# The first MLP product of a two-block layer by seven quarter products instead of eight

## The chip, the core and the metric

The kernel runs on one core of a Trainium2 chip. The metric is device time in microseconds (us) of one execution. The core has a matrix engine (TensorE, here PE), VectorE (DVE), ScalarE (ACT), GpSimd (POOL) and queues of DMA transfers, here all issued by SyncE (SP). Each engine takes its instructions in a fixed order; semaphores make one wait for another.

## What is computed

Two blocks on x of 1024 tokens by 1024 channels, all in fp32. The part around the change is the MLP of block 1 and what follows it:

```python
h = rms_norm(x, g_mlp[l])
f = jnp.square(jax.nn.relu(jnp.einsum("bsd,df->bsf", h, w_1[l])))   # 1024 -> 4096
x = x + jnp.einsum("bsf,fd->bsd", f, w_2[l])                         # 4096 -> 1024
...
x = rms_norm(x, g_final)                                             # end of block 1
...
h = rmsnorm(x, norm_g[l]); proj = h @ w_in[l]                        # block 2
...
mn = rmsnorm(mem, mem_norm_g); kv = mn @ w_kv                        # memory attention, 256 rows of mem
```

## The kernel before

Activations lie with channels on the 128 partitions and tokens along the free axis, in two halves of 512 tokens (`hf`). Every fp32 matrix product is made of three passes in a 22-bit form of fp32: each operand is split into a high part H (rounded, by ACT) and a low part L (the rest, by DVE), and L·H, H·L and H·H are summed in PSUM. So a tile of 128 output channels by 512 tokens with a contraction of 1024 takes 8 x 3 = 24 matmuls of 128x128 on 128x512.

`weight` (L101 on) loads a weight tile of 128x1024 (512 KB, L106) into one of two staging buffers `wst`, has ACT write its high part `wh` (L108) and DVE its low part `wl` (L110); four `wh` and four `wl` buffers turn. `split` does the same for activations (ACT L131, DVE L132). `mm3` issues the matmuls: all cross passes first (L124), then H·H (L127), or operand by operand when `ordered` (L119). Accumulators in PSUM have the tags `pm` and `pa`, four buffers each.

`out_proj` ends with the RMS norm of the MLP's input, half by half: squares (ACT L152), their sum over tiles (DVE L155), the sum over partitions by two matmuls (`spread`, L167 and L168), the reciprocal root (`rsqrt`: ACT L176, L179, DVE L181, L184, L186), then `scaled`: for each of eight channel tiles one multiplication (DVE L194) and a split into the pages `acth` and `actl`.

`mlp` runs over eight groups `e` of 512 inner channels. For each half it makes four tiles of the first product, takes relu out of PSUM on ACT (L636), squares on DVE (L638) and splits into the pages `e0` to `e7`; then, with four tiles of `w_2`, 16 output tiles of 12 matmuls, each added to x on DVE (L648). In the last group the sums of squares for the norms of block 1's end and block 2's start follow each add (L152, L155), and after each half come the norm, the scaled and split input of block 2, and, at low priority, x scaled and written to DRAM (L660, L661). Ahead of group 6 `mem_norm` (its sums at L882, its scaling at L873) normalizes the memory rows; the kv product of those rows (weights `w_kv`) stands after the MLP and before the projection of block 2.

A list scheduler fixes the order of each engine's instructions by priorities: weights are given the place they would have 185 instructions earlier (`W_AHEAD`), the relu and the adds are moved up by 500 (`urgent`), the writing of x back by 300 (`LATE`). Where buffers of a tag are all in use, an instruction waits for the last reader of the oldest.

Of the kernel before, what the change touches and what calls it, by code (L numbers as in the profile page):

```python
# [61 lines left out]
class Builder:  # L62
# [36 lines left out]
    def urgent(self):  # L99
        return self.tc.high_priority(offset=URGENT)  # L100

# [490 lines left out]
    def out_proj(self, mx):  # L592
        nc, V = self.nc, self.nc.vector
        self.x1 = [None] * 8
        h2 = Act(KC)
        acc = [None, None]
        for b in range(2):
            ws = [self.weight(self.io["w_o"][4 * b + i]) for i in range(4)]
            for hf in range(2):
                sl = slice(hf * HALF, (hf + 1) * HALF)  # L600
                for i in range(4):
                    c = 4 * b + i
                    if hf == 0:
                        self.x1[c] = self.page(f"x{c}")
                    xr = self.load(self.io["x"][c][:, sl])
                    ps = self.ct(ws[i], mx, hf)
                    V.tensor_tensor(self.x1[c][:, sl], ps, xr, ALU.add)  # L607
                    acc[hf] = self.square_sum(acc[hf], self.x1[c][:, sl])
                if b == 1:
                    rs = self.rsqrt(self.spread(acc[hf], self.mean_d), EPS)  # L610
                    self.scaled(h2, hf, [t[:, sl] for t in self.x1], self.vec("g_mlp", 0, KC), rs)
        return h2

    def ct4(self, w, j, act, hf, first=0, cols=slice(0, HALF)):
        ps = self.psum((P, cols.stop - cols.start))
        h, l = w
        self.mm3(ps, [(h[:, j * HALF + k * P:j * HALF + (k + 1) * P], l[:, j * HALF + k * P:j * HALF + (k + 1) * P],
                       act.H(hf, first + k)[:, cols], act.L(hf, first + k)[:, cols]) for k in range(4)])
        return ps

    def mlp(self, h2):
        nc, V, A = self.nc, self.nc.vector, self.nc.scalar
        h3 = Act(KC)
        for e in range(8):
            if e == 6:
                self.mem = self.mem_norm()
            f = Act(4)
            ws = [self.weight(self.io["w_1"][4 * e + i]) for i in range(4)]
            for hf in range(2):
                for pr in range(2):  # L630
                    self.ext_pages(f, hf, pr, hf * 4 + pr)
                for i in range(4):
                    ps = self.ct(ws[i], h2, hf, e == 0 and i == 0)
                    t = self.tmp("b")
                    with self.urgent():
                        A.activation(t, ps, AF.Relu)  # L636
                    t2 = self.tmp("b")
                    V.tensor_tensor(t2, t, t, ALU.mult)  # L638
                    self.split(t2, f.H(hf, i), f.L(hf, i))
            w2 = [self.weight(self.io["w_2"][4 * e + i]) for i in range(4)]  # L640
            for hf in range(2):
                sl = slice(hf * HALF, (hf + 1) * HALF)
                acc1 = acc2 = None
                for c in range(8):
                    ps = self.ct4(w2[c // 2], c % 2, f, hf)
                    x = self.x1[c][:, sl]
                    with self.urgent():
                        V.tensor_tensor(x, ps, x, ALU.add)  # L648
                    if e == 7:
                        acc1 = self.square_sum(acc1, x)  # L650
                        acc2 = self.square_sum(acc2, x, self.vec("g_final", c))
                if e == 7:
                    V.scalar_tensor_tensor(acc2, acc1, EPS, acc2, ALU.mult, ALU.add)
                    rs = self.rsqrt(self.spread(acc2, self.mean_d), EPS * EPS)
                    self.scaled(h3, hf, [t[:, sl] for t in self.x1], self.gg, rs)
                    rs1 = self.rsqrt(self.spread(acc1, self.mean_d), EPS, out=acc1)
                    with self.tc.high_priority(offset=-LATE):
                        for c in range(8):
                            x = self.x1[c][:, sl]
                            V.scalar_tensor_tensor(x, x, self.vec("g_final", c), rs1, ALU.mult, ALU.mult)  # L660
                            nc.sync.dma_start(self.x_dram[c][hf], x)  # L661
        return h3

    def gates(self, h3):
        nc, V, A, G = self.nc, self.nc.vector, self.nc.scalar, self.nc.gpsimd
# [370 lines left out]
    def build(self):  # L1036
        tc = self.tc
        MT = bass.MemoryType
        with (
            tc.tile_pool(name="consts", bufs=1) as self.consts,  # L1040
            tc.tile_pool(name="smalls", bufs=8) as self.smalls,
            tc.tile_pool(name="wst", bufs=2) as self.wst,
            tc.tile_pool(name="wh", bufs=N_W) as self.wh,
            tc.tile_pool(name="wl", bufs=N_W) as self.wl,
            tc.tile_pool(name="pages", bufs=1) as self.pages,
            tc.tile_pool(name="rolls", bufs=N_ROLL) as self.rolls,
            ExitStack() as stack,
            tc.tile_pool(name="dram", bufs=1, space=MT.DRAM) as dram,
        ):
# [9 lines left out]
            self.x_dram = [[dt("xd", 2 * c + hf, (P, HALF)) for hf in range(2)] for c in range(8)]  # L1059
            self.rows_dram = [[dt("rows", 2 * i + hf, (4, HALF)) for hf in range(2)] for i in range(2)]  # L1060
# [12 lines left out]
LATE = 300  # L1073
URGENT = 500
CONV_STEP = 20
N_ROLL = 2
# [20 lines left out]
def _ct_groups(w):  # L1097
    k, c = w.shape
    return w.reshape(k // HALF, 4, P, c // 256, 2, P).transpose(0, 3, 2, 4, 1, 5).reshape(-1, P, 1024)


def _layout(a):
    o = {}
# [13 lines left out]
    o["w_rg"] = wr.reshape(4, P, 1024)  # L1117
    o["w_o"] = _ct(a["w_o"][0])
    o["w_1"] = _ct(a["w_1"][0])
    o["w_2"] = _ct_groups(a["w_2"][0])  # L1120
    w2 = a["w_in_2"][0]
    gates = np.zeros((D, P), np.float32)
    gates[:, 0:4] = w2[:, 2560:2564]
# [10 lines left out]
    for n, c in V_COLS:  # L1134
# [6 lines left out]
        elif n in ("conv_a_w", "conv_b_w", "conv_w_2"):  # L1141
            w = a[n][0][:, RNN_ORDER] if n == "conv_b_w" else a[n][0]
# [55 lines left out]
```

## Time and profile before

| | |
|---|---|
| median of 3 runs | 2385.77 us (2385.24 to 2388.82) |
| profiled execution, its time | 2385.94 us |
| its span in the trace | 2384.2 us |
| PE / DVE / ACT busy | 98% / 63% / 37% |
| MLP, first to last matmul | 986.69 to 1684.98 us |

Busy shares are means over stages with different limits; a stage is read from its own stretch. In a timeline, the brackets tell how long the engine stood idle before an instruction and what released it. A row that stands for several instructions (x3) shows the time from the first's start to the last's end, and these overlap somewhat: their start-to-start time is shorter than the time of one.

### The profile page before, as it was taken

The page shows a single profiled execution, that of the slowest core. Times are in us where ns is not written, and L with a number is a line of the kernel's source. Part 1 is how long each engine was busy: PE and PEld are TensorE (multiplying, and loading weights), DVE is VectorE, ACT ScalarE, POOL GpSimd, SP SyncE. Part 2 cuts the span into 40 slices and gives each one's busy share as a digit, 9 for nine tenths or more (in the row PEclk, how much of TensorE's full clock was granted, in tenths as well). Part 3 has the DMA queues.
Part 4 walks back from the last instruction along what each step waited for, and adds up shares of the span by engine and source line. Part 5 has one row for each costly group of instructions (what it writes and reads, how often), then busy time and mean ns, then how long its engine had stood idle before and what let it go on. Part 6 is the DMA issues. An engine that isn't in the chain of part 4 may idle for free.

```text
span 2384.2 us, 26982 instructions
## 1 busy us (share of the span) xinstructions
PE 2341.8 (98%) x10656; PEld 1934.1 (81%) x10656; DVE 1498.1 (63%) x2233; ACT 883.9 (37%) x1370; POOL 18.8 (1%) x44
## 2 busy tenths in 40 slices
PE   8999999999999999999999999999899999999998
PEld 6887888878878888888888888888787888888777
DVE  8999998995664234743343333435937467775866
ACT  6445463555552112422112212314614344443422
POOL 0000000000000000000000000000000000000000
PEclk9999999999999999999999999999999999999999
DMA  4223232233425223211121121111322111223421
GB/s 155 80 67 98 66 91 90 83 105 101 136 89 174 82 81 105 78 54 53 36 62 45 45 62 36 53 53 36 112 101 63 54 58 53 81 65 109 133 88 71
DMA packets 76480, 191.09 MB, mean 80 GB/s; under 512 B 9264, under 2 KB 11824, under 8 KB 76352
## 3 DMA queue, kind: packets, MB, share of 16 engines
q1 hardware_dynamic: 76352, 189.36, 25.2%
q8 instruction: 83, 1.36, 0.2%
q14 instruction: 45, 0.37, 0.1%
HBM read 153.64 MB, written 34.11 MB: 79 GB/s over the span
## 4 chain that ended last, share of the span: by engine, by line
PE 72%; DVE 9%; ACT 2%; issue 2%; DMA 1%; POOL 0%; DVEq 0%; ACTq 0%; POOLq 0%
PE pm L124 45%; PE pm L127 22%; PE pa L124 2%; DVE e L358 1%; DVE wl L110 1%; PE pa L127 1%; DMA ld<-y 1%; DVE actl L132 1%; DVE row L155 1%; ACT wh L108 0%; DVE c L194 0%; DVE x L1033 0%; ACT c L152 0%; PE pa L802 0%; PE pa L948 0%
## 5 line engine op out<-in xcount | busy, mean ns | idle before, releaser
L124 PE MATMUL pm<-acth,wl 128*128 128x512 f32 (+1 forms) x2480 | 960.2, 388 | 9.8 <-ACT b L473 5.5
L124 PE MATMUL pm<-actl,wh 128*128 128x512 f32 (+1 forms) x2480 | 960.3, 388 | 0.4 <-DVE actl L132 0.4
L127 PE MATMUL pm<-acth,wh 128*128 128x512 f32 (+1 forms) x2480 | 620.9, 387 | 0.0
L124 PEld LDWEIGHTS pm<-acth,wl 128*128 128x128 f32 x2480 | 466.7, 188 | 106.8 <-ACT b L473 6.8
L124 PEld LDWEIGHTS pm<-actl,wh 128*128 128x128 f32 x2480 | 466.9, 188 | 96.2 <-DVE actl L132 1.7
L127 PEld LDWEIGHTS pm<-acth,wh 128*128 128x128 f32 x2480 | 461.8, 188 | 93.6 <-issue 0.7
L108 ACT ACTIVATE wh<-wst 128x1024 fp32r<-128x1024 f32 x209 | 220.5, 1057 | 543.2 <-PE pm L127 516.2
L110 DVE TENSOR_TENSOR wl<-wst,wh 128x1024 fp32r<-128x1024 f32 x209 | 255.3, 1224 | 87.9 <-ACT wh L108 87.3
L124 PE MATMUL pm<-e,wl 128*128 128x512 f32 x592 | 230.4, 389 | 0.0
L124 PE MATMUL pm<-e,wh 128*128 128x512 f32 x592 | 230.3, 389 | 0.0
L648 DVE TENSOR_TENSOR x<-pm,x 128x512 f32<-128x512 f32 x128 | 88.5, 691 | 176.2 <-PE pm L127 176.1
L127 PE MATMUL pm<-e,wh 128*128 128x512 f32 x592 | 158.1, 389 | 0.0
L638 DVE TENSOR_TENSOR b<-b 128x512 f32<-128x512 f32 x64 | 44.4, 693 | 177.6 <-ACT b L636 177.6
L124 PEld LDWEIGHTS pm<-e,wl 128*128 128x128 f32 x592 | 111.1, 188 | 23.4 <-DVE wl L110 0.4
L127 PEld LDWEIGHTS pm<-e,wh 128*128 128x128 f32 x592 | 111.1, 188 | 23.1
L124 PEld LDWEIGHTS pm<-e,wh 128*128 128x128 f32 x592 | 111.1, 188 | 23.1
L358 DVE SCALAR_TENSOR_TENSOR e<-roll,pv,e 128x507 f32<-128x507 f32 (+14 forms) x174 | 120.5, 748 | 0.0
L636 ACT ACTIVATE b<-pm 128x512 f32<-128x512 f32 x64 | 38.4, 599 | 203.5 <-PE pm L127 202.7
L358 DVE SCALAR_TENSOR_TENSOR e<-roll,tap_sum,e 128x511 f32<-128x511 f32 (+14 forms) x90 | 63.2, 746 | 0.0
L152 ACT ACTIVATE c<-x 128x512 f32<-128x512 f32 (+1 forms) x63 | 36.1, 580 | 70.5 <-DVE x L607 35.0
L155 DVE TENSOR_TENSOR row<-row,c 128x512 f32<-128x512 f32 (+1 forms) x77 | 48.2, 642 | 15.6 <-ACT c L152 15.5
L579 DVE TENSOR_TENSOR b<-pm,ld 128x512 f32<-128x512 f32 x16 | 11.0, 690 | 71.7 <-PE pm L127 71.7
(313 smaller groups left out, 2301.5 us busy)
## 6 DMA issues: line engine op xcount, KB each, us to landing
wst<-in_w_in SPq DMA_DIRECT2D x89, 512.0 KB, 3.5
wst<-in_w SPq DMA_DIRECT2D x64, 512.0 KB, 3.5
sig<-b SPq DMA_DIRECT2D x32, 256.0 KB, 2.8
ld<-sig SPq DMA_DIRECT2D x32, 256.0 KB, 2.6
a<-p SPq DMA_DIRECT2D x24, 256.0 KB, 3.9
wst<-in_w_b_out SPq DMA_DIRECT2D x12, 512.0 KB, 4.2
y<-b SPq DMA_DIRECT2D x24, 256.0 KB, 2.0
wst<-in_w_out SPq DMA_DIRECT2D x12, 512.0 KB, 3.5
```

The lines of the kernel that those rows point to most:

```text
L108: nc.scalar.activation(h, st, AF.Copy)
L110: nc.vector.tensor_tensor(l, st, h.bitcast(F32), ALU.subtract)
L124: self.nc.tensor.matmul(ps, a, b, start=i == 0, stop=i == n - 1)
L127: self.nc.tensor.matmul(ps, aH, bH, start=i == 0, stop=i == n - 1)
L132: self.nc.vector.tensor_tensor(L, srcap, H.bitcast(F32), ALU.subtract)
L152: nc.scalar.activation(sq, x, AF.Square, scale=scale)
L155: (eng or nc.vector).tensor_tensor(acc, acc, sq, ALU.add)
L358: ops.append(lambda k=k: V.scalar_tensor_tensor(out[:, k:], x[:, :HALF - k], taps[k], out[:, k:], ALU.mult, ALU.add))
L579: V.tensor_tensor(t, ps, sg, ALU.mult)
L636: A.activation(t, ps, AF.Relu)
L638: V.tensor_tensor(t2, t, t, ALU.mult)
L648: V.tensor_tensor(x, ps, x, ALU.add)
```

## The change

The first 512 inner channels are done as before. The other 3584 come in 14 steps `q` of 256. In a step the first product, 256 inner channels by 1024 by 1024 tokens, is taken as a 2x2 by 2x2 block product (two tiles of channels, two halves of the contraction, two halves of the tokens) and made by seven block products of 12 matmuls instead of eight (`seven`, `product`). They need sums of the operands and of the results:

- Four sums of activation blocks, T1 to T4, 16 tiles of 128x512. They are made once, while half 1 of the normalized x is scaled (`scaled_and_sums`, six operations for each of four pairs of tiles), written to DRAM (`t_dram`, 16 tiles of 256 KB), and, during the first 512 channels, read again and split (`sum_pair`). T2 and T3 then fill the working tiles `a`, `c`, `roll` and `ld` and T1 and T4 fill pages until the last step.
- Four sums of weight blocks per step (`weight_sums`, DVE), and the high and low parts of 3584 instead of 2048 columns of `w_1` material.
- Seven combinations of the products per step, read out of PSUM by DVE, and one copy by ACT, instead of four relus by ACT. The square is one DVE operation, max(z, 0)·z.

The second product of a step has a contraction of 256: 16 output tiles of 6 matmuls, each with an add to x, where a group had 16 tiles of 12. The host stores `w_2` in another order for it. `mem_norm`, whose tiles are held by the sums, comes after the seven products of the last step. In the last step the output tiles of half 0 come before those of half 1, with the norms as before.

```diff
+    def scaled_and_sums(self, act, xs, g, rs):
...
+        def one(k):
+            ts[k] = self.tmp("c")
+            V.scalar_tensor_tensor(ts[k], xs[k], g[:, k:k + 1], rs, ALU.mult, ALU.mult)
+            self.split(ts[k], act.H(1, k), act.L(1, k))
...
+        for k in range(4):
+            one(k)
+            one(4 + k)
+            with self.tc.high_priority(offset=-SUMS_LATE):
+                t12, t22 = ts.pop(k), ts.pop(4 + k)
+                t1 = self.tmp("c")
+                V.tensor_tensor(t1, act.H(0, k).bitcast(F32), t12, ALU.subtract)
+                V.tensor_tensor(t1, t1, act.L(0, k).bitcast(F32), ALU.add)
+                nc.sync.dma_start(self.t_dram[0][k], t1)
+                V.tensor_tensor(t12, t12, t22, ALU.subtract)
+                nc.sync.dma_start(self.t_dram[2][k], t12)
+                V.tensor_tensor(t22, t22, t1, ALU.add)
+                nc.sync.dma_start(self.t_dram[1][k], t22)
+                t4 = self.tmp("c")
+                V.tensor_tensor(t4, act.H(0, 4 + k).bitcast(F32), t22, ALU.subtract)
+                V.tensor_tensor(t4, t4, act.L(0, 4 + k).bitcast(F32), ALU.add)
+                nc.sync.dma_start(self.t_dram[3][k], t4)
+    def sum_pair(self, i, k, homes):
...
+        t = self.tmp("row")
+        nc.sync.dma_start(t, self.t_dram[i][k])
+        self.split(t, homes[0], homes[1])
...
+    def weight_sums(self, s1, s0):
...
+            st1 = self.wst.tile([P, 1024], F32, tag="wst", name=self.name("wst"))
+            nc.sync.dma_start(st1, s1)
+            st0 = self.wst.tile([P, 1024], F32, tag="wst", name=self.name("wst"))
+            nc.sync.dma_start(st0, s0)
...
+            a1 = parts(st1)
+            a22 = parts(st0[:, hi], 512)
+            V.tensor_tensor(st0[:, hi], st0[:, lo], st0[:, hi], ALU.add)
+            V.tensor_tensor(st0[:, lo], st1[:, lo], st0[:, lo], ALU.add)
+            V.tensor_tensor(st1[:, lo], st0[:, hi], st1[:, lo], ALU.add)
+            V.tensor_tensor(st1[:, hi], st1[:, lo], st1[:, hi], ALU.add)
+            x24 = parts(st1)
+            x31 = parts(st0)
...
+        p1 = self.product(w["A11"], B["B11"])
...
+            A.activation(c11, p1, AF.Copy)
+        p6 = self.product(w["X2"], B["T2"])
...
+        tt(c12, c11, p6, ALU.subtract)
+        p4 = self.product(w["A22"], B["T4"])
+        p7 = self.product(w["X3"], B["T3"])
...
+        tt(c22, p7, c12, ALU.subtract)
...
+        tt(c21, p4, c22, ALU.add)
+        p5 = self.product(w["X1"], B["T1"])
+        tt(c22, c22, p5, ALU.subtract)
+        tt(c12, c12, p5, ALU.add)
+        p2 = self.product(w["A12"], B["B21"])
+        tt(c11, c11, p2, ALU.add)
+        p3 = self.product(w["X4"], B["B22"])
+        tt(c12, c12, p3, ALU.add)
...
+        for q in range(2, 16):
+            w = self.weight_sums(self.io["w_1"][2 * q], self.io["w_1"][2 * q + 1])
...
+            c11, c12, c21, c22 = self.seven(w, B)
+            self.squared(c21, None, fh[0][1], fl[0][1])
+            self.squared(c11, None, fh[0][0], fl[0][0])
+            self.squared(c22, None, fh[1][1], fl[1][1])
+            self.squared(c12, None, fh[1][0], fl[1][0])
+            if q == 15:
                 self.mem = self.mem_norm()
...
+            w2 = [self.weight(self.io["w_2"][2 * q + j]) for j in range(2)]
+            for hf, b in ((0, 0), (1, 0), (0, 1), (1, 1)) if q < 15 else ((0, 0), (0, 1), (1, 0), (1, 1)):
...
+                    x = self.add_x(c, hf, ps)
+                    if q == 15:
+                        acc[0] = self.square_sum(acc[0], x)
+                        acc[1] = self.square_sum(acc[1], x, self.vec("g_final", c))
+                if q == 15 and b == 1:
+                    self.norm2(hf, *acc)
```

Three places in the order of the engines' instructions show what moved. The first is DVE where half 1 of the normalized x is scaled; `c` are the scaled tiles and the sums, `acth` and `actl` the pages of the normalized x, `b` squares of the first group. Before:

```order
L186 SCALAR_TENSOR_TENSOR c_7627<-c_7628,c_7627 128x512
L194 SCALAR_TENSOR_TENSOR c_7636<-x_1024_7040,pv,c_7627 128x512
L194 SCALAR_TENSOR_TENSOR c_7640<-x_1028_7071,pv,c_7627 128x512
L194 SCALAR_TENSOR_TENSOR c_7646<-x_1032_7103,pv,c_7627 128x512
L132 TENSOR_TENSOR actl_1119_7635<-c_7636,acth_1118_7634 128x512
L132 TENSOR_TENSOR actl_1119_7635<-c_7640,acth_1118_7634 128x512
L132 TENSOR_TENSOR actl_1123_7645<-c_7646,acth_1122_7644 128x512
L194 SCALAR_TENSOR_TENSOR c_7650<-x_1036_7135,pv,c_7627 128x512
```

After:

```order
L626 SCALAR_TENSOR_TENSOR c_7658<-x_1024_7056,pv,c_7643 128x512
L626 SCALAR_TENSOR_TENSOR c_7662<-x_1064_7330,pv,c_7643 128x512
L636 TENSOR_TENSOR c_7666<-acth_1085_7472,c_7658 128x512
L132 TENSOR_TENSOR actl_1119_7651<-c_7658,acth_1118_7650 128x512
L132 TENSOR_TENSOR actl_1123_7655<-c_7662,acth_1122_7654 128x512
L637 TENSOR_TENSOR c_7666<-c_7666,actl_1086_7473 128x512
L639 TENSOR_TENSOR c_7658<-c_7658,c_7662 128x512
L804 TENSOR_TENSOR b_7821<-b_7821 128x512
L641 TENSOR_TENSOR c_7662<-c_7662,c_7666 128x512
L804 TENSOR_TENSOR b_7851<-b_7851 128x512
L644 TENSOR_TENSOR c_7674<-acth_1093_7492,c_7662 128x512
L626 SCALAR_TENSOR_TENSOR c_7678<-x_1028_7087,pv,c_7643 128x512
```

Eight scalings and splits stood together; now six sums (L636 to L645) stand behind each pair of scalings (L626) and ahead of the next pair.

The second is ACT at the change from the first to the second product. Before, in a group of 512 channels (`b` a relu or its square, `e` pages, `wh` high parts of weights):

```order
L636 ACTIVATE b_7917<-pm_7892 128x512
L108 ACTIVATE wh_7968<-wst_7966 128x1024
L131 ACTIVATE e_1164_7828<-b_7919 128x512
L636 ACTIVATE b_7948<-pm_7923 128x512
L108 ACTIVATE wh_7974<-wst_7972 128x1024
L131 ACTIVATE e_1164_7828<-b_7950 128x512
L108 ACTIVATE wh_8204<-wst_8202 128x1024
```

After, in a step of 256 (`pa` is the first of the seven products; L108 are tiles of `w_2`, L671 of the next step's `w_1` sums):

```order
L709 ACTIVATE b_8385<-pa_8372 128x512
L108 ACTIVATE wh_8489<-wst_8487 128x1024
L131 ACTIVATE e_1254_8368<-b_8430 128x512
L108 ACTIVATE wh_8495<-wst_8493 128x1024
L671 ACTIVATE wh_8631<-wst_8627 128x1024
L131 ACTIVATE e_1255_8369<-b_8428 128x512
L671 ACTIVATE wh_8635<-wst_8629 128x512
L131 ACTIVATE e_1254_8368<-b_8385 128x512
L131 ACTIVATE e_1255_8369<-b_8400 128x512
```

Three high parts of the next step's weights and of `w_2` now stand between the step's four splits of squares (L131).

The third is DVE behind the last tiles of the MLP's second product; `pm` is an accumulator, `row` and `c` sums of squares, and L110 the first low parts of `w_kv`. Before:

```order
L648 TENSOR_TENSOR x_1076_7410<-pm_12130,x_1076_7410 128x512
L132 TENSOR_TENSOR actl_1759_11953<-c_11954,acth_1758_11952 128x512
L132 TENSOR_TENSOR actl_1759_11953<-c_11958,acth_1758_11952 128x512
L132 TENSOR_TENSOR c_11963<-row_11763,c_11962 128x512
L110 TENSOR_TENSOR wl_12276<-wst_12272,wh_12274 128x1024
L110 TENSOR_TENSOR wl_12309<-wst_12305,wh_12307 128x1024
```

After:

```order
L810 TENSOR_TENSOR x_1076_7426<-pm_12544,x_1076_7426 128x512
L155 TENSOR_TENSOR row_12261<-row_12261,c_12301 128x512
L155 TENSOR_TENSOR row_12263<-row_12263,c_12304 128x512
L155 TENSOR_TENSOR row_12261<-row_12261,c_12315 128x512
L155 TENSOR_TENSOR row_12263<-row_12263,c_12318 128x512
L155 TENSOR_TENSOR row_12261<-row_12261,c_12329 128x512
L155 TENSOR_TENSOR row_12263<-row_12263,c_12332 128x512
L110 TENSOR_TENSOR wl_12651<-wst_12647,wh_12649 128x1024
L155 TENSOR_TENSOR row_12261<-row_12261,c_12343 128x512
```

Six additions of squares now stand between the last add to x and the first low part of `w_kv`, where two activation splits and one of the norm stood.

## Rows read from the trace of the kernel before

**Rows 1.** The page: busy times by engine, and the chain that ended last.
```profile
PE 2341.8 (98%) x10656; PEld 1934.1 (81%) x10656; DVE 1498.1 (63%) x2233; ACT 883.9 (37%) x1370; POOL 18.8 (1%) x44
...
PE 72%; DVE 9%; ACT 2%; issue 2%; DMA 1%; POOL 0%; DVEq 0%; ACTq 0%; POOLq 0%
PE pm L124 45%; PE pm L127 22%; PE pa L124 2%; DVE e L358 1%; DVE wl L110 1%; PE pa L127 1%; DMA ld<-y 1%; DVE actl L132 1%; DVE row L155 1%; ACT wh L108 0%; DVE c L194 0%; DVE x L1033 0%; ACT c L152 0%; PE pa L802 0%; PE pa L948 0%
```
**Rows 2.** By stretch: us, PE, PEld, DVE, ACT, POOL busy, PEclk, DMA share, GB/s.
```profile
1080.24:1167.28 87.04, 87.04 (x385) 72.10 (x384) 31.51 (x40) 17.46 (x25) 0.00 (x0) 1.00 0.16 49
1684.98:1720.97 35.99, 27.89 (x149) 23.85 (x147) 35.15 (x53) 22.99 (x37) 0.00 (x0) 0.86 0.43 139
```
**Rows 3.** Timeline of PE, MLP steady state: start us, us, engine line op names xcount.
```profile
1096.36 0.39 PE L124 MATMUL pm<-acth,wl 128*128 128x512 f32 x1
...
1101.80 0.39 PE L124 MATMUL pm<-acth,wl 128*128 128x512 f32 x1
```
**Rows 4.** Groups by line, 990 to 1684.98: line engine op xcount | busy us, mean ns.
```profile
L110 DVE TENSOR_TENSOR wl<-wst,wh 128x1024 fp32r<-128x1024 f32 x61 | 74.8, 1225 | 20.4 <-ACT wh L108 20.4
...
L132 DVE TENSOR_TENSOR e<-b,e 128x512 fp32r<-128x512 f32 x64 | 44.1, 689 | 18.9 <-ACT e L131 18.9
L131 ACT ACTIVATE e<-b 128x512 fp32r<-128x512 f32 x64 | 40.1, 627 | 21.4 <-DVE b L638 21.3
...
L132 DVE TENSOR_TENSOR a<-c,roll 128x256 fp32r<-128x256 f32 x8 | 3.0, 425 | 0.0
```
**Rows 5.** Waits, 990 to 1684.98: engine line <- releaser: us in total, times, longest.
```profile
ACT wh L108 <- PE pm L127: 273.8, 30, 25.1
...
DVE x L648 <- PE pm L127: 176.1, 107, 2.0
```
**Rows 6.** DMA issues of the page: names, queue, xcount, KB each, us to landing.
```profile
wst<-in_w SPq DMA_DIRECT2D x64, 512.0 KB, 3.5
sig<-b SPq DMA_DIRECT2D x32, 256.0 KB, 2.8
ld<-sig SPq DMA_DIRECT2D x32, 256.0 KB, 2.6
...
wst<-in_w_b_out SPq DMA_DIRECT2D x12, 512.0 KB, 4.2
```
**Rows 7.** Timeline, half 1 of the normalized x: DVE, then PE, then PE's next stage.
```profile
997.76 0.69 DVE L184 SCALAR_TENSOR_TENSOR c<-c,c 128x512 f32<-128x512 f32 x1
998.49 0.69 DVE L186 SCALAR_TENSOR_TENSOR c<-c,c 128x512 f32<-128x512 f32 x1
999.22 2.08 DVE L194 SCALAR_TENSOR_TENSOR c<-x,pv,c 128x512 f32<-128x512 f32 x3
1001.21 1.89 DVE L132 TENSOR_TENSOR actl<-c,acth 128x512 fp32r<-128x512 f32 x3
...
1009.32 0.39 PE L119 MATMUL pm<-acth,wl 128*128 128x512 f32 x1
...
1031.08 0.39 PE L124 MATMUL pm<-e,wl 128*128 128x512 f32 x1
```
**Rows 8.** Timeline, from the MLP to block 2: PE, then DVE.
```profile
1684.98 0.28 PE L124 MATMUL pm<-roll,wl 128*128 128x256 f32 x1
...
1706.18 0.76 PE L124 MATMUL pm<-wh,a 128*128 128x512 f32 x1 [4.94 <-DVE e L132]
...
1708.65 0.63 PE L124 MATMUL pm<-wl,roll 128*128 128x512 f32 x1
1709.08 0.63 PE L124 MATMUL pm<-wh,a 128*128 128x512 f32 x1
...
1710.65 0.39 PE L124 MATMUL pm<-wh,a 128*128 128x512 f32 x1
...
1720.97 0.50 PE L124 MATMUL pm<-acth,wl 128*128 128x512 f32 x1 [1.05 <-DVE wl L110]
...
1687.59 2.35 DVE L110 TENSOR_TENSOR wl<-wst,wh 128x1024 fp32r<-128x1024 f32 x2
```

More of the change, by code (lines that the diff above doesn't have):

```diff
@@ new lines, in product, with seven, tt @@
+    def product(self, a, b):
+        ps = self.psum(tag="pa")
+        n = 0
+        for passes in (((1, 0), (0, 1)), ((0, 0),)):
+            for (aH, aL), (bH, bL) in zip(a, b):
+                for i, j in passes:
+                    self.nc.tensor.matmul(ps, (aH, aL)[i], (bH, bL)[j], start=n == 0, stop=n == 11)
+                    n += 1
+        return ps
+    def seven(self, w, B):
+        V, A = self.nc.vector, self.nc.scalar
+        def tt(out, a, b, op):
+            with self.urgent():
+                V.tensor_tensor(out, a, b, op)
+        p1 = self.product(w["A11"], B["B11"])
+        c11 = self.tmp("b")
+        with self.urgent():
+            A.activation(c11, p1, AF.Copy)
+        p6 = self.product(w["X2"], B["T2"])
+        c12 = self.tmp("b")
+        tt(c12, c11, p6, ALU.subtract)
+        p4 = self.product(w["A22"], B["T4"])
+        p7 = self.product(w["X3"], B["T3"])
+        c22 = self.tmp("b")
+        tt(c22, p7, c12, ALU.subtract)
+        c21 = self.tmp("b")
+        tt(c21, p4, c22, ALU.add)
[6 more added lines that the diff above has]
+        tt(c12, c12, p3, ALU.add)
+        return c11, c12, c21, c22
@@ L622, in mlp @@
         nc, V, A = self.nc, self.nc.vector, self.nc.scalar
-        h3 = Act(KC)
-        for e in range(8):
-            if e == 6:
-                self.mem = self.mem_norm()
[L627 to L661, printed above, removed]
@@ L662, in mlp @@
-        return h3
+        self.h3 = Act(KC)
+        f = Act(4)
+        ws = [self.weight(self.io["w_1"][i]) for i in range(4)]
+        for hf in range(2):
+            for pr in range(2):
+                self.ext_pages(f, hf, pr, hf * 4 + pr)
+            for i in range(4):
+                ps = self.ct(ws[i], h2, hf, i == 0)
+                t = self.tmp("b")
+                with self.urgent():
+                    A.activation(t, ps, AF.Relu)
+                self.squared(t, t, f.H(hf, i), f.L(hf, i))
@@ new lines, in mlp, with squared, add_x, norm2 @@
+        return self.h3
+    def squared(self, z, relu, H, L):
+        V = self.nc.vector
+        if relu is None:
+            V.scalar_tensor_tensor(z, z, 0.0, z, ALU.max, ALU.mult)
+        else:
+            V.tensor_tensor(z, relu, relu, ALU.mult)
+        self.split(z, H, L)
+    def add_x(self, c, hf, ps):
+        x = self.x1[c][:, hf * HALF:(hf + 1) * HALF]
+        with self.urgent():
+            self.nc.vector.tensor_tensor(x, ps, x, ALU.add)
+        return x
+    def norm2(self, hf, acc1, acc2):
+        nc, V = self.nc, self.nc.vector
+        sl = slice(hf * HALF, (hf + 1) * HALF)
+        V.scalar_tensor_tensor(acc2, acc1, EPS, acc2, ALU.mult, ALU.add)
+        rs = self.rsqrt(self.spread(acc2, self.mean_d), EPS * EPS)
+        self.scaled(self.h3, hf, [t[:, sl] for t in self.x1], self.gg, rs)
+        rs1 = self.rsqrt(self.spread(acc1, self.mean_d), EPS, out=acc1)
+        with self.tc.high_priority(offset=-LATE):
+            for c in range(8):
+                x = self.x1[c][:, sl]
+                V.scalar_tensor_tensor(x, x, self.vec("g_final", c), rs1, ALU.mult, ALU.mult)
+                nc.sync.dma_start(self.x_dram[c][hf], x)
@@ L1059, in build @@
             self.x_dram = [[dt("xd", 2 * c + hf, (P, HALF)) for hf in range(2)] for c in range(8)]
+            self.t_dram = [[dt("t", 4 * i + k, (P, HALF)) for k in range(4)] for i in range(4)]
             self.rows_dram = [[dt("rows", 2 * i + hf, (4, HALF)) for hf in range(2)] for i in range(2)]
@@ L1073 @@
 LATE = 300
+SUMS_LATE = 60
 URGENT = 500
```

62 lines of the change are left out of this document (60 added, 2 removed).

## The prediction

> **What bounds the kernel now.** I read the page first. TensorE (PE) is busy for 2341.8 of 2384.2 us, and the chain that ended last runs through PE for 72%, 67 points of it in the two lines of the three-pass product, L124 and L127 [rows 1]. Then the stretches of the MLP by engine: in a stage of 512 channels, 384 matmuls, PE is busy for all of 87.04 us at granted clock 1.00 (the 2.4 GHz level), while VectorE (DVE) has 31.51 us of work and ScalarE (ACT) 17.46 [rows 2]. So a matmul left out there is worth its start-to-start time. 24 of them lie between 1096.36 and 1101.80 [rows 3]: 5.44 / 24 = 0.2267 us each. The table of waits says the same from the other side: ACT and DVE wait for PE (273.8 and 176.1 us) [rows 5], and PE for nothing large. Two places differ: ahead of half 1 of the first group, and between the last MLP matmul (1684.98) and the first projection matmul of block 2 (1720.97), where DVE is busy for 35.15 of 35.99 us, PE for 27.89, and the granted clock is 0.86 [rows 2, 8].
>
> **What is removed.** Each of 14 steps has seven quarter products of 12 matmuls in place of eight: 14 x 12 = 168 matmuls x 0.2267 = **-38.1 us**. Everything else of the change is work for DVE, ACT and the queues, and costs only what PE comes to wait for. The Trainium skill, "TensorE: Matmul & The Clock Gate", section Back-to-back issue gap, gives a sustained 131 ns for a 512-column matmul; by that the saving would be 22 us only. The trace disagrees (0.2267), and the trace decides.
>
> **A step of 256 channels, on DVE.** The two relu-and-square passes become one operation each, but the number of adds to x per channel doubles (16 per 256 channels instead of 16 per 512), and there come four weight sums, seven combinations out of PSUM and 3584 columns of weight parts instead of 2048 for w_1. One step: 16 adds, 4 sums, 7 combinations, 4 squares, 4 splits = 35 operations of 512 columns at 0.69, half a weight split at 0.69, and five whole ones at 1.225 [rows 4] = 31 us. PE needs 180 x 0.2267 = 40.8 us. Before, half of 31.51, or 15.8 us, stood beside 43.5 [rows 2]. DVE goes from 36% to 76%: it still fits, so the mean costs nothing; what can cost is order.
>
> I followed one step by hand, T = 0 at the end of its seventh product. The last split of w_2 (L110) can only start after the fifth product, whose weight buffers it takes (T = -5.44), and two combinations precede it on DVE: it ends at about -2.8. Only then is the staging buffer free and SP can issue the next step's second w_1 tile, which lands 3.5 us later [rows 6], at +0.7. ACT's order puts the high part of this tile (512 columns, 0.63 as L131 [rows 4]) ahead of the high parts of two squares; the first of those comes out at 2.1 with its handovers, and PE wants it for the 11th matmul after the product, at 2.3. On DVE the low part of the same square stands behind the tile's low part, another split and a sum and ends at 4.3 to 4.5; PE wants it for the 19th, at 4.1. Queued behind the waiting ACT instruction are both splits, and behind them on PE the rest of the group. So 0.2 to 0.5 us a step, 0.4 taken; with every handover at its shortest 0.1; with a landing as slow as the 4.2 of another weight queue [rows 6] the high part is late by 0.5 and drags the adds with it, about 1.0. Thirteen such steps: **+5 us** (1 to 13). Nothing else in the step came out late: the weight sums end near T = 10 and are multiplied from T = 24 on, and the adds free the four accumulators about 0.3 us ahead of PE.
>
> **Entry: the sums of the activations.** Half 1 of the normalized x was scaled by 8 L194 and split by 8 L132, on DVE from 999.22 to about 1010, just as PE came to it at 1009.32 [rows 7]. Now six sums stand behind each pair. The order of DVE has 37 operations between the start of scaling and the pair of the last index: 6 scalings (0.66 apart: 2.08 for three overlapping ones), 31 others at 0.60 (three in 1.89) [rows 7] = 22.6 us. So that pair starts at about 1021.8, and its high part reaches PE at about 1023.5. In PE's order 27 of the 96 matmuls of half 1 stand before this wait; 69 x 0.2267 = 15.6 us follow, and end at 1039.1 against 1031.08 [rows 7]: 8 us late. PE idles about 2 and then 5.7 us before. After an idle stretch of 4.94 us the trace of before shows 512-column matmuls 0.43 apart until 1710.65 [rows 8], where the full level comes back: ten or so, 2 us more. **+10 us** (8 without the slow matmuls, 13 with two such runs of them and a late low part). Spilling and reloading 4 MB each way is hidden: DMAs of 256 KB take 2.6 to 2.8 us to land [rows 6], and the sums are first multiplied after the 43.5 us of the first group's second product, under which their 16 splits (11 us of DVE at 0.69) lie.
>
> **Exit: the last second product.** It was 16 groups of 12 matmuls (43.5 us), and is 16 of 6 (21.8 us). Under it DVE has to do what it did before per group (one add, two L155) and now the memory norm too: its tiles hold the activation sums until the seventh products are done. DVE's order shows the result: after the last add six L155 stand ahead of the first split of w_kv, which begins the kv product. 0.6 + 6 x 0.6 + 1.14 = 5.4 us of idle PE plus handovers, 6 in all, where before the kv product followed at once [rows 8]. From there on DVE sets the pace: up to the split that the projection waits for there are 24 L155 and 10 L132 at 0.60, 9 L110 at 1.13 [rows 8], 8 L194 at 0.66, 6 dependent operations of the two norms at 0.73 [rows 7] and 4 short splits at 0.42 [rows 4]: 42 us, and 3 to 6 of waits for ACT and PE. The projection starts some 48 us after the last MLP matmul; before it was 36.0 [rows 8]. +12, and 2 for its half 1, whose norm is as late: **+14 us** (9 if the waits overlap, 20 if slow matmuls and late kv weights add to it; no gain, since DVE was the busy engine there already and gets more to do).
>
> Sum against the profiled execution's own 2385.94 (span 2384.2; median of the runs 2385.77, so nothing to correct): -38.1 + 5 + 10 + 14 = -9.1, **2377 us**. All bounds on one side: 2366 and 2394.
>
> **Rivals.** *Clean gain.* If PE's sequencer finds every operand in time in the steps, and the entry costs the slow matmuls alone and the exit 2: -38.1 + 4 = 2352. For it: 64% of DVE's time in a stage is idle [rows 2]. Against it: the orders above, which are fixed. 12%.
> *Gain eaten, no change* (2381 to 2391): stalls of 0.8 to 1.4 us a step, or an exit of over 20. For it: the step's chain crosses SP, DMA, ACT and DVE in turn, and I gave each handover its fast value. 22%.
> *Slower: the staging buffer paces the step.* The same chain, with the tile landing 1.5 to 2 us later than PE wants it in all 13 steps: the high part of the square, then the low part, then the accumulators slip together. At 2 us: -38.1 + 26 + 10 + 14 = +12, 2398. It decides from (38.1 - 24 + 4.8) / 13 = 1.45 us a step. Against it: 3.5 us is a steady median [rows 6] and the stall I find is 0.4. 11%.
> That PE doesn't get fewer matmuls is excluded: its order has 168 fewer.
> By the Trainium skill's 131 ns (same page and section) the first term would be -22.0 and the time 2393, slower. A stage of 384 matmuls in 87.04 us [rows 2] leaves that no chance of its own; it lies inside the 11%.
>
> **How the numbers follow.** The forecast, 2366 to 2381, has 55%; with the clean gain 67% faster by over 0.2% (about what a measurement of this kernel can tell from no change; 4.8 us), 22% within, 11% slower. The range 2358 to 2392 leaves out the better part of the clean case, some 10%, and most of the slower one, some 9%.
>
> **What would show it.** Right: PE near 100% busy in the steps, 41.0 to 41.5 us apart, with one wait of PE each for ACT's or DVE's split of a square near the change to w_2; two waits for ACT's acth split near 1014 and 1018, the longer 5 to 6 us; a wait for the first wl of w_kv after the last MLP matmul of 5 to 7 us and 46 to 50 us to the projection. Wrong: steps over 42.3 us apart (the slower rival), or under 40.9 with no such waits (the clean one); an entry under 5 us or an exit under 5 us would say that the hand-followed order of DVE overstates the queue.

## The result, and the profile after

The changed kernel takes 2370.8 us (median, 2369.21 to 2372.94) against 2386.1 us before, in runs on one chip: the ratio is 0.9935, with a 95% interval of 0.9917 to 0.9952. It is faster by 15.3 us, 0.65%. The forecast was 2377 us, 9.1 us faster.

The page of the changed kernel, busy times by engine (the row of [rows 1]):

```profile
PE 2308.9 (97%) x10488; PEld 1901.5 (80%) x10488; DVE 1707.5 (72%) x2567; ACT 895.7 (38%) x1372; POOL 18.6 (1%) x44
```

PE has 168 matmuls less and 32.9 us less busy time; DVE has 209.4 us more (1498.1 before). Its span is 2368.7 us, 15.5 less. Starts of the same work in the two traces divide this difference. The first MLP matmul is the first L119 of `mlp`; "first w_2" is the first matmul of the first group's second product; the rest of the MLP begins, after the change, with the first step of 256 channels; "block 2" is the first projection matmul. The MLP ends where PE goes on to the next matmul or begins to wait for it.

| stretch | before, us | after, us | difference |
|---|---|---|---|
| start to first MLP matmul | 986.69 | 988.68 | +2.0 |
| first MLP matmul to first w_2 | 44.39 | 54.89 | +10.5 |
| second product of the first group | 43.52 | 43.52 | 0 |
| rest of the MLP | 610.38 | 573.32 | -37.1 |
| last MLP matmul to block 2 | 35.99 | 47.08 | +11.1 |
| block 2 to the end | 663.23 | 661.21 | -2.0 |
| sum | 2384.2 | 2368.7 | -15.5 |

**The steps.** Busy time by stretch of the changed kernel: all 14 steps, and then the exit (us, PE, PEld, DVE, ACT, POOL busy, PEclk, DMA share, GB/s; rows as in [rows 2]):

```profile
1087.09:1660.41 573.32, 573.32 (x2523) 471.59 (x2521) 413.09 (x598) 138.33 (x182) 0.00 (x0) 1.00 0.17 53
1660.41:1707.49 47.08, 29.21 (x149) 24.70 (x148) 43.15 (x65) 31.55 (x50) 0.00 (x0) 0.82 0.28 89
```

PE has no idle time of note in 573.32 us, at full granted clock, with DVE busy for 413.09, 72%, where it had 36% in a stage of the kernel before. 14 x 180 matmuls at 0.2267 us are 571.2 us, so all waits of PE in 14 steps come to about 2 us.

The table of waits from 960 to 1800 us (engine, line <- releaser: us in total, times, longest), as in [rows 5]:

```profile
DVE x L810 <- PE pm L127: 60.0, 89, 2.0
...
ACT wh L671 <- DMA wst<-in_w: 14.7, 13, 1.2
...
PEld pm L119 <- ACT e L131: 2.7, 13, 0.2
```

DVE still waits for PE with its adds, but 60.0 us instead of 176.1, and ACT waits 13 times, about once a step, for the landing of a tile of w_1. PE's weight loads (PEld) wait 13 times too, 0.2 us each, for the high part of a square of the step; the matmuls themselves show no wait over 0.15 us.

**The entry.** Timeline of PE (start us, us, engine line, operation, names; in brackets the idle time and its releaser), as in [rows 7]:

```profile
988.68 0.39 PE L119 MATMUL pm<-acth,wl 128*128 128x512 f32 x1
...
1011.18 0.39 PE L119 MATMUL pm<-acth,wl 128*128 128x512 f32 x1
...
1017.29 0.50 PE L119 MATMUL pm<-acth,wl 128*128 128x512 f32 x1 [1.87 <-ACT acth L131]
...
1025.23 0.79 PE L119 MATMUL pm<-acth,wl 128*128 128x512 f32 x1 [5.32 <-ACT acth L131]
...
1029.59 0.63 PE L119 MATMUL pm<-acth,wh 128*128 128x512 f32 x1
...
1030.40 0.39 PE L119 MATMUL pm<-actl,wh 128*128 128x512 f32 x1
...
1043.57 0.39 PE L124 MATMUL pm<-e,wl 128*128 128x512 f32 x1
```

Half 1 begins at 1011.18, 22.5 us after the first MLP matmul as before. Then PE stands twice, 1.87 and 5.32 us, for the high part of a scaled tile that ACT makes out of what DVE delivers late. Behind the second wait matmuls stand 0.43 us apart (1029.59, next 1030.02) until about 1030.40.

**The exit.** Timeline of PE, as in [rows 8]:

```profile
1659.80 0.61 PE L127 MATMUL pm<-e,wh 128*128 128x512 f32 x2
...
1666.03 0.55 PE L124 MATMUL pm<-roll,wl 128*128 128x256 f32 x1 [5.62 <-DVE wl L110]
...
1691.15 0.79 PE L167 MATMUL pa<-c,mean_d 128*128 128x512 f32 x1 [7.86 <-DVE c L132]
...
1700.60 0.50 PE L124 MATMUL pm<-wl,roll 128*128 128x512 f32 x1 [2.26 <-DVE wl L110]
...
1707.49 0.50 PE L124 MATMUL pm<-acth,wl 128*128 128x512 f32 x1 [1.61 <-DVE wl L110]
```

The first split of w_kv holds PE for 5.62 us, the sum over partitions of a norm for 7.86, other splits of weights for 2.26 and 1.61. DVE is busy for 43.15 of the 47.08 us.

### The profile page after: what moved, and what is told of

Same layout as the page of the kernel before. It is cut to its first block, busy times and chain, and to the rows that moved or that the text cites. A ratio compares the mean times of both kernels' runs of the same rounds, so it can differ in the third digit from the quotient of the medians.

```text
span 2368.7 us, 27112 instructions
## 1 busy us (share of the span) xinstructions
PE 2308.9 (97%) x10488; PEld 1901.5 (80%) x10488; DVE 1707.5 (72%) x2567; ACT 895.7 (38%) x1372; POOL 18.6 (1%) x44
## 5 line engine op out<-in xcount | busy, mean ns | idle before, releaser
L124 PE MATMUL pm<-acth,wl 128*128 128x512 f32 (+1 forms) x2032 | 784.7, 388 | 10.9 <-ACT b L473 6.0
L124 PE MATMUL pm<-actl,wh 128*128 128x512 f32 (+1 forms) x2032 | 785.0, 388 | 0.5 <-DVE actl L132 0.4
L127 PE MATMUL pm<-acth,wh 128*128 128x512 f32 (+1 forms) x2032 | 509.9, 386 | 0.0
L124 PEld LDWEIGHTS pm<-acth,wl 128*128 128x128 f32 x2032 | 382.5, 188 | 90.4 <-ACT b L473 7.3
L124 PEld LDWEIGHTS pm<-actl,wh 128*128 128x128 f32 x2032 | 382.4, 188 | 79.4 <-DVE actl L132 2.5
L127 PEld LDWEIGHTS pm<-acth,wh 128*128 128x128 f32 x2032 | 377.3, 188 | 76.0 <-issue 0.7
L108 ACT ACTIVATE wh<-wst 128x1024 fp32r<-128x1024 f32 x181 | 190.7, 1056 | 334.0 <-PE pm L127 237.5
L110 DVE TENSOR_TENSOR wl<-wst,wh 128x1024 fp32r<-128x1024 f32 x181 | 220.2, 1219 | 112.1 <-ACT wh L108 111.0
L810 DVE TENSOR_TENSOR x<-pm,x 128x512 f32<-128x512 f32 x240 | 160.9, 689 | 74.6 <-PE pm L127 60.0
L671 ACT ACTIVATE wh<-wst 128x1024 fp32r<-128x1024 f32 (+1 forms) x56 | 53.5, 955 | 262.2 <-PE pm L127 226.5
L695 PE MATMUL pa<-acth,wl 128*128 128x512 f32 x224 | 87.3, 390 | 0.0
L695 PE MATMUL pa<-actl,wh 128*128 128x512 f32 x224 | 87.2, 389 | 0.0
L119 PE MATMUL pm<-e,wh 128*128 128x512 f32 x256 | 79.8, 396 | 0.6 <-DVE e L275 0.6
L131 ACT ACTIVATE e<-b 128x512 fp32r<-128x512 f32 x64 | 40.4, 632 | 101.5 <-DVE b L802 97.0
L705 DVE TENSOR_TENSOR b<-b,pa 128x512 f32<-128x512 f32 x70 | 46.8, 685 | 37.4 <-PE pa L695 36.4
```

Source lines behind the costliest of these rows:

```text
L108: nc.scalar.activation(h, st, AF.Copy)
L110: nc.vector.tensor_tensor(l, st, h.bitcast(F32), ALU.subtract)
L119: self.nc.tensor.matmul(ps, a, b, start=i == 0, stop=i == n - 1)
L124: self.nc.tensor.matmul(ps, a, b, start=i == 0, stop=i == n - 1)
L127: self.nc.tensor.matmul(ps, aH, bH, start=i == 0, stop=i == n - 1)
L131: self.nc.scalar.activation(H, srcap, AF.Copy)
```

## The experiments

Theory: the 168 matmuls save their 38.1 us, the steps cost next to nothing, and two places take 21.6 us back, the entry by the place of the sums in DVE's order, the exit by the halved cover of the last second product (cover: the work of PE under which DVE does what the next stage needs). The rivals are told with each run. Each kernel was timed on one chip beside the kernel before, whose median was 2386.6 or 2386.7 us there, against 2386.1 above; differences from the changed kernel's 2370.8 hold to about that 0.6 us.

### The sums behind the first product

```diff
-                        self.scaled_and_sums(h2, xs, self.vec("g_mlp", 0, KC), rs)
+                    self.scaled(h2, hf, xs, self.vec("g_mlp", 0, KC), rs)
...
+    def sums(self, act, rs):
...
         for k in range(4):
...
+            t12, t22 = again(k), again(4 + k)
...
+        self.sums(h2, self.rs_mlp)
```

`sums` is called in `mlp` behind the first product of the first group, and `again` makes the two scalings once more.

> The six sums per pair are emitted behind the first group's first product instead of between the scalings of half 1; scaling and splitting there is as before the change, and the sums scale their eight tiles a second time (8 more DVE operations). Theory (the order of DVE at the entry costs 10.5 us: the waits of 1.87 and 5.32 us for acth and the slow matmuls after them): the entry goes back to about 44.4 us from the first MLP matmul to the first matmul with w_2, and the time to about 2361. Rival (the volume of the sums costs, not their place): DVE has some 65 us of work in the 65 us from half 1 to the first step, so PE waits for split sums (T2, T4) in the first step instead, by 5 to 10 us, and the time stays at 2366 to 2371.

It took 2359.69 us (ratio to the kernel before 0.9887, interval 0.9872 to 0.9902), 11.1 less than the changed kernel. Timeline of PE, the first MLP matmul, the first with w_2, then the exit:

```profile
987.99 0.39 PE L119 MATMUL pm<-acth,wl 128*128 128x512 f32 x1
...
1032.35 0.39 PE L124 MATMUL pm<-e,wl 128*128 128x512 f32 x1
...
1655.50 0.55 PE L124 MATMUL pm<-roll,wl 128*128 128x256 f32 x1 [5.62 <-DVE wl L110]
...
1696.44 0.50 PE L124 MATMUL pm<-acth,wl 128*128 128x512 f32 x1 [1.61 <-DVE wl L110]
```

From 987.99 to 1032.35 are 44.36 us, before the change 44.39: the entry is back whole, though DVE does eight more scalings, and no wait of PE over 0.2 us came up in the first step. From the first kv matmul (it waits for 5.62 us again) to the projection little changed: 40.94 us here, 41.46 there. So the place costs, not the volume: the rival's 5 to 10 us of waits did not come (the 14 steps take 0.7 us more).

### The last two second products joint

```diff
         for q in range(2, 16):
...
+            if q == 15:
+                fh = [self.halves(t) for t in ("e0", "e1")]
+                fl = [self.halves(t) for t in ("e2", "e3")]
...
+            pair.append((fh, fl))
+            if q == 14:
+                continue
...
-                    self.mm3(ps, [(w2[b][0][:, o[k]], w2[b][1][:, o[k]], fh[hf][1 - k], fl[hf][1 - k]) for k in range(2)],
-                             j == 0)
+                    self.mm3(ps, [(w[b][0][:, o[k]], w[b][1][:, o[k]], p[0][hf][1 - k], p[1][hf][1 - k])
+                                  for w, p in zip(w2, pair) for k in range(2)], j == 0 and q < 15)
```

> The last two steps do their first products one after the other, and their second products jointly, with a contraction of 512: the last 16 output tiles have 12 matmuls each again (43.5 us), at the same number of matmuls in all; mem_norm stays behind the last seven products. Theory (the exit costs because the cover for adds, squares and norms was halved): from the last MLP matmul to the first projection matmul 36 to 38 us instead of 47.1, less about 1.2 us of PE waiting for the weight sums between the two steps; the time about 2362. Rival (mem_norm standing in the exit is the cost): the exit stays over 44 us and the time within 2 us of 2371.

It took 2362.64 us (0.99, 0.9885 to 0.9914). Timeline of PE:

```profile
1599.14 0.50 PE L695 MATMUL pa<-a,wl 128*128 128x512 f32 x1 [1.08 <-DVE wl L672]
...
1660.00 0.28 PE L124 MATMUL pm<-roll,wl 128*128 128x256 f32 x1
...
1685.12 0.77 PE L124 MATMUL pm<-wh,a 128*128 128x512 f32 x1 [7.58 <-DVE e L132]
...
1700.44 0.50 PE L124 MATMUL pm<-acth,wl 128*128 128x512 f32 x1 [1.05 <-DVE wl L110]
```

Busy time from the kv product to the projection:

```profile
1660.00:1700.44 40.44, 28.68 (x149) 24.31 (x147) 37.95 (x57) 25.20 (x40) 0.00 (x0) 0.83 0.37 124
```

The kv product follows the MLP without a wait, and the exit takes 40.44 us: 6.6 less than in the changed kernel, more than the 36 to 38 that the theory wanted, less than the 44 of the rival. The 1.08 us for a weight sum between the two steps is the wait that was expected. So the cover explains the larger part of what the exit cost, 6.6 of 11.1 us, and not all.

### The memory rows scaled early

```diff
         self.x1 = [None] * 8
+        self.mem_early()
...
     def mem_norm(self):
...
+        for i in range(4):
+            r = self.tmp("c", shape=(P, 2, N_MEM))
+            self.nc.sync.dma_start(r, self.m_dram[i])
+            self.split(r, mH[i // 2][:, i % 2 * 2:i % 2 * 2 + 2, :], mL[i])
```

`mem_early` makes the sums of squares and the scaling, ahead of `out_proj`, and writes four tiles to DRAM.

> The sums of squares and the scaling of the memory rows are done ahead of out_proj and the scaled rows written to DRAM; at the old place behind the last seven products they are only read and split (four splits of 512 columns for eight of 256). Theory (halved cover; mem_norm is a minor part): DVE has about 4.5 us less to do under the last second product, so the exit falls from 47.1 to about 42.5 us and the time to about 2366. Rival (mem_norm is the exit's cost): the exit falls to about 36 us and the time to about 2360.

It took 2363.19 us (0.99, 0.9884 to 0.9917). Timeline of PE: the first kv matmul, the first wait behind it, the projection:

```profile
1657.89 0.28 PE L124 MATMUL pm<-roll,wl 128*128 128x256 f32 x1
...
1661.78 0.39 PE L124 MATMUL pm<-roll,wl 128*128 128x256 f32 x1 [0.85 <-DVE wl L110]
...
1699.43 0.50 PE L124 MATMUL pm<-acth,wl 128*128 128x512 f32 x1 [1.60 <-DVE wl L110]
```

The exit takes 41.54 us, 5.5 less; the theory had 42.5, the rival 36. But 5.5 of 11.1 us is half, not the minor part that the theory called it. The time lies 2.8 us under the forecast, halfway to the rival's 2360: the rest of the gain is in the MLP (the first of the two waits at the entry is 0.85 us here in place of 1.87, and the entry takes 53.11 us; why was not tried).

### Eight products in the same steps

```diff
-            c11, c12, c21, c22 = self.seven(w, B)
-            self.squared(c21, None, fh[0][1], fl[0][1])
...
+            ws = [self.weight(self.io["w_1"][2 * q + i]) for i in range(2)]
+            for hf in range(2):
+                for i in (1, 0):
+                    ps = self.ct(ws[i], h2, hf)
...
+                    self.squared(t, t, fh[hf][i], fl[hf][i])
```

The sums of activations and weights are gone, and `mem_norm` stands ahead of the last two steps.

> Steps of 256 channels as in the changed kernel, but the first product by eight quarter products in the usual way (192 matmuls a step, relu by ACT, no sums of activations or weights); mem_norm ahead of the last two steps. Theory (a matmul is worth its 0.2267 us; entry and exit are the only other large terms): +38.1 for the 168 matmuls, -10.5 for the entry, -0.9 for the steps, and an exit shorter by the 4.5 us of mem_norm: about 2393, that is, some 7 us slower than the kernel before, all of it at the exit. Rival (a matmul is worth 0.131 us, or DVE paced the steps of seven): the 168 matmuls cost 22 us or less, and the time is below 2378.

It took 2390.22 us (1.0016, 1.0007 to 1.0026): slower than the kernel before by about 4 us, not 7. Timeline of PE, first MLP matmul, first w_2, first kv matmul, projection:

```profile
986.39 0.39 PE L119 MATMUL pm<-acth,wl 128*128 128x512 f32 x1
...
1030.70 0.39 PE L124 MATMUL pm<-e,wl 128*128 128x512 f32 x1
...
1683.77 0.28 PE L124 MATMUL pm<-roll,wl 128*128 128x256 f32 x1
...
1725.77 0.50 PE L124 MATMUL pm<-acth,wl 128*128 128x512 f32 x1 [1.40 <-DVE wl L110]
```

The entry is 44.31 us. The steps last from 1030.70 + 43.52 = 1074.22 to 1683.77, 609.55 us, and with seven products 573.32: the 168 matmuls are worth 36.2 us in the trace, their 38.1 less the 2 us of waits of the steps of seven. The exit is 42.00 us, 6.0 more than before, with the memory norm out of it. The 3 us missed lie in the stretch from block 2 to the end (661.1 us against 663.2 before) and in 0.8 us of the steps.

All runs, with those below, give the exit for either cover and either place of the memory norm (from the last MLP matmul to the projection, us). With the early rows only the sums and the scaling are ahead; four loads and splits stay in the exit:

| | norm ahead | norm in the exit |
|---|---|---|
| 43.5 us of cover | 35.99 (before), 37.07 (all three) | 40.44 (joint), 40.80 (two together) |
| 21.8 us of cover | 42.00 (eight products), 41.54 (early rows) | 47.08 (changed kernel), 46.56 (sums behind), 44.60 (second copy) |

The halved cover costs 3.8 to 6.6 us, the memory norm 2.6 to 5.5, and together they are the 11.1. The second copy's kernel has the cover and the norm of the changed one and still an exit 2.5 us shorter, by another order of DVE there. So the two shares are known to within some 3 us, and what the order of the exit alone is worth was not tried.

### A second copy in the step's chain

```diff
-                nc.scalar.activation(h[:, :n], src, AF.Copy)
+                for _ in range(times):
+                    nc.scalar.activation(h[:, :n], src, AF.Copy)
...
-            a22 = parts(st0[:, hi], 512)
+            a22 = parts(st0[:, hi], 512, 2)
```

> In each of the 14 steps ACT makes the high part of the late w_1 tile (512 columns) twice in a row, which adds about 0.53 us to the chain that the prediction followed from the landing of that tile to the high part of the square. Theory (the chain ends just when PE wants the square: in the changed kernel's trace the high part is ready at 2.15 us and PE wants it at 2.26 us after the last of the seven products, so only about 0.1 us is left): 0.4 to 0.5 us more a step, 13 to 14 times, +5 to +7 us, about 2377. Rival (the step has slack of a microsecond or more, the prediction followed a chain that is not the last to end): no change, 2371.

It took 2372.61 us (0.9944, 0.9927 to 0.9961), between the two and within the spread of the changed kernel's runs. Timeline of ACT, the doubled copy and the high part of the square behind it, then of PE (the first step, a change to the second product, the last MLP matmul's successor):

```profile
1186.82 1.30 ACT L672 ACTIVATE wh<-wst 128x512 fp32r<-128x512 f32 x2 [1.07 <-DMA wst<-in_w]
1188.02 0.62 ACT L131 ACTIVATE e<-b 128x512 fp32r<-128x512 f32 x1
...
1084.96 0.39 PE L696 MATMUL pa<-acth,wl 128*128 128x512 f32 x1
...
1186.09 0.39 PE L119 MATMUL pm<-e,wl 128*128 128x512 f32 x1
...
1188.13 0.39 PE L696 MATMUL pa<-acth,wl 128*128 128x512 f32 x1
...
1188.69 0.49 PE L119 MATMUL pm<-e,wl 128*128 128x512 f32 x1
...
1661.24 0.28 PE L124 MATMUL pm<-roll,wl 128*128 128x256 f32 x1
```

The 14 steps take 1661.24 - 1084.96 = 576.28 us, 3.0 more than in the changed kernel, 0.21 a step. (In two kernels without the copy they take 572.8, early rows, and 574.0, sums behind, so the 3.0 is good to about 1 us.) Neither forecast came: not 0.4 to 0.5 a step, and not nothing.

What became of the delay can be followed. Two copies take 1.30 us and one 0.63, so it is 0.66, not the 0.53 expected. From the change to the second product (1186.09) until PE takes the square are 2.60 us here, 2.57 to 2.86 over 13 steps, instead of 2.27 in the changed kernel: 0.41 later in the mean. So the tile's chain had 0.66 - 0.41, about 0.25 us, in hand. Of the 0.41 the step lost only 0.21, since the scheduler put two matmuls of the next step's product (1188.13 and its successor) ahead of the one that waits, where the changed kernel has one; a matmul fills 0.23. With the order as it was, the step would have lost about 0.4, by this sum; no run shows it.

The run isn't clean in two more points: DVE's order at this place changed too, and the exit is 44.60 us instead of 47.08, which is why the time shows little of the 3.0.

### Two and three of them together

These are the edits above, joined.

> The sums behind the first group's first product (as in e1) and the last two second products joint (as in e2) together. Theory (entry and exit are separate costs and add): 2359.7 - 6.7 + 1.9 to 2359.7 - 8, so 2352 to 2355. Rival (the two share a limit, DVE's total work in the MLP, 72% and more of the span): less than half of the second gain, over 2357.

2351.36 us (0.9854, 0.984 to 0.9869): the gains add. Timeline of PE, first kv matmul and projection, an exit of 40.80 us:

```profile
1649.03 0.28 PE L124 MATMUL pm<-roll,wl 128*128 128x256 f32 x1
...
1689.83 0.50 PE L124 MATMUL pm<-acth,wl 128*128 128x512 f32 x1 [1.05 <-DVE wl L110]
```

> The sums behind the first product, the joint last second product, and the memory rows scaled ahead of out_proj, together. Theory (with the cover back, what is left of the exit over the kernel before, 40.4 against 36.0 us, is mem_norm): 3 to 4 us less than without the early memory rows, 2348 to 2351. Rival (with 43.5 us of cover the 7 us of mem_norm are hidden, and the rest of the exit is something else): within 1 us of the kernel with the first two.

2349.88 us (0.9848, 0.9833 to 0.9862), 1.5 less in the median. Timeline of PE, first kv matmul and projection:

```profile
1650.93 0.28 PE L124 MATMUL pm<-roll,wl 128*128 128x256 f32 x1
...
1688.00 0.50 PE L124 MATMUL pm<-acth,wl 128*128 128x512 f32 x1 [1.05 <-DVE wl L110]
```

The exit is 37.07 us, 3.7 less than with two, as the theory had it, and 1.1 from the kernel before. In the time only 1.5 us show of the 3 to 4 that were expected. In the two profiled executions the reason lies ahead of the MLP: the first MLP matmul is at 988.08 here and at 985.98 with two (last section). Whether that holds for the other executions of the two kernels isn't shown. This version is 21 us faster than the changed kernel and 36 us faster than the one before.

## Why the prediction was right, and where it was off

The direction was right, and the time lies inside the range: -9.1 forecast, -15.3 measured. The forecast gain was 6 us too small: the steps were put 4 us too dear and the exit 3, the entry half a microsecond too cheap. Two differences that no term foresaw, +2.0 ahead of the MLP and -2.0 behind block 2's start, cancel in the profiled executions by luck. The terms:

- **The removed matmuls**, -38.1: right. A step of 180 matmuls takes 573.32 / 14 = 40.95 us. The 131 ns of the Trainium skill ("TensorE: Matmul & The Clock Gate", Back-to-back issue gap), by which the saving would have been 22 us, is not what these pairs of weight load and matmul show: 609.55 us for 14 x 192 matmuls without sums are 0.2268 each.
- **The entry**, +10: right, +10.5. Two waits were forecast at 2 and 5.7 us, measured 1.87 and 5.32, and the slow matmuls behind the second one came. By parts, the waits came out at 7.2 us (8 forecast) and the rest at 3.3 (2 forecast). Undoing the place of the sums gave back the whole of it.
- **The exit**, +14: the mechanism was right, the size a little high, +11.1. The first wait was forecast at 6 us and is 5.62; the projection starts 47.1 us after the MLP, not 48. The 2 us for half 1 of the projection did not come: the profile has no wait of PE over 0.2 us in the first 60 us of it. The prediction took half 1's norm to be as late as half 0's and, as far as its text tells, did not follow what PE has to do with half 0 before it wants half 1.
- **The steps**, +5: the mis-sized term. About 2.1 us of waits in 14 steps, 0.15 each; the kernel before had 1.1 in the same stretch, so the net is +1.0, the lower end of 1 to 13. The steps are 40.89 to 40.94 us apart, just under the 41.0 to 41.5 given as the sign, with the wait for a square that was part of it. Here is the chain that was followed, in one step of the changed kernel: DVE's last split of w_2, SP's issue, ACT's high part of the late tile and of the square, DVE's low part of the square, and then PE's first, 11th and 19th matmul after the seven products. The last three rows are a second chain, DVE's combination and square of a product and the weight load of the 11th matmul:

```profile
1183.87 1.22 DVE L110 TENSOR_TENSOR wl<-wst,wh 128x1024 fp32r<-128x1024 f32 x1
...
1185.12 0.33 SPq L666 DMA_DIRECT2D wst<-in_w  x1
...
1188.68 0.63 ACT L671 ACTIVATE wh<-wst 128x512 fp32r<-128x512 f32 x1 [1.12 <-DMA wst<-in_w]
...
1189.43 0.63 ACT L131 ACTIVATE e<-b 128x512 fp32r<-128x512 f32 x1
...
1191.15 0.69 DVE L132 TENSOR_TENSOR e<-b,e 128x512 fp32r<-128x512 f32 x1
...
1187.91 0.39 PE L119 MATMUL pm<-e,wl 128*128 128x512 f32 x1
...
1190.17 0.44 PE L119 MATMUL pm<-e,wl 128*128 128x512 f32 x1
...
1192.08 0.63 PE L119 MATMUL pm<-e,wh 128*128 128x512 f32 x2
...
1188.11 0.69 DVE L705 TENSOR_TENSOR b<-b,pa 128x512 f32<-128x512 f32 x1
1188.71 0.69 DVE L802 SCALAR_TENSOR_TENSOR b<-b 128x512 f32<-128x512 f32 x1
...
1190.12 0.19 PEld L119 LDWEIGHTS pm<-e,wl 128*128 128x128 f32 x1 [0.21 <-ACT e L131]
```

With T = 0 at 1187.91, the split of w_2 ends at -2.8 as forecast (1183.87 + 1.22), the tile is there at +0.77 (forecast 0.7), the square's high part at 2.15 (2.1) and PE takes it at 2.26 (2.3). Wrong was the other branch, which the 0.4 us a step rested on: the low part ends at 1191.15 + 0.69, 3.93, not 4.3 to 4.5. PE wants it at 4.17 and does not wait. Four operations of DVE from the tile's low part on lead to that end; they start 0.60 apart and last 0.69 each, so four durations in a row would be 0.26 us too long. That is over half of the miss at its lower end; the rest lies in handovers that the prediction does not itemize.

The prediction also did not follow the chain that ended last. ACT is done with the tile's high part at 1188.68 + 0.63 = 1189.31 and stands until DVE's square ends at 1188.71 + 0.69 = 1189.40. That square waits in DVE's order behind the combination L705, which takes up the seventh product. In 13 steps the tile's high part ends 1.33 to 1.50 us after T, and the square's high part starts at 1.52 each time, so the tile's landing had 0.02 to 0.19 us to spare. What PE's weight load waits for, 0.21 us here, is the chain over DVE. That the forecast of 2.1 for the high part was met is luck in this respect.

The range of 2358 to 2392 was wide on the slow side for want of this: the rival by which the staging buffer paces the step, at 2398, would have needed 2 us a step, and 1.45 to be slower at all; even a deliberate delay of 0.66 us cost the step 0.21.

What stays open: 2.0 us less from block 2 to the end. All later kernels have it (659.8 to 661.9 us against 663.23), the one with eight products too, so it doesn't need the seven products. The waits of PE behind the first projection matmul sum to 6.6 us against 8.1; the kernel before has one of 1.72 us, 504 us into block 2, for a high part that ACT makes, and the changed kernel has none there. Why that wait is gone was not tried.

## What to carry over

Work that an engine has room for on average still costs what stands behind it in its queue: sums that were due 60 us later stood ahead of splits that PE needed at once, and moving them behind gave back 11 us for 0.7 us in the steps. Before a stage that hides something else (norms, loads) is made shorter, count what it hides: the saving of a product does not carry over into the stretch where another engine sets the pace. To price a chain in a full queue, use start-to-start intervals for every link, and handovers only where the engine has been idle; and follow every chain that ends at the instruction in question, for the one that was not followed can be the last.

## What was not expected of the hardware

The start of the MLP differs by 2 us between profiled executions of nearly the same work: 986.0 to 986.7 us in five (before, joint, second copy, eight products, two together), 988.0 to 988.7 in four (changed, sums behind, early rows, all three). Busy time by stretch, 500 to 560 us, of the kernel before:

```profile
500.00:560.00 60.00, 59.42 (x262) 49.14 (x263) 48.78 (x59) 27.18 (x35) 0.00 (x0) 1.00 0.39 124
```

and of the changed kernel:

```profile
500.00:560.00 60.00, 59.12 (x253) 48.77 (x254) 49.13 (x59) 26.10 (x34) 0.00 (x0) 0.97 0.38 122
```

PE waits for some 2.5 us at the start of this stretch in both (2.65 us until 500.58 before, 2.53 until 500.88 after). In one the granted clock stays at 1.00, in the other it is 0.97 over the stretch, without a longer wait, and from the end of the wait to the first MLP matmul it takes 487.80 us instead of 486.11, 1.7 more. The other executions fall in line: over 500 to 560 us the granted clock is 1.00 in all five of the early group and 0.97 in all four of the late one. At a like wait at 212 us it is the other way round in these two: 0.97 over 205 to 265 us before, 1.00 after. So a wait of 2.5 us costs its own length in some executions and 1.7 us more in others, and a difference of 2 us between two single executions here says nothing on the change. Over the entry, with its wait of 5.32 us, the changed kernel's granted clock is 0.94, the kernel before's 1.00.
